# Twelve input-projection blocks taken in pairs by seven half-size products instead of eight

## The chip, the core and the metric

The kernel runs on one core of a Trainium2 chip. Its engines work side by side and are held together by semaphores: PE (TensorE, matrix products; PEld is its loading of the stationary operand), DVE (VectorE), ACT (ScalarE), POOL (GpSimd) and SP, which issues most DMA transfers. Products are written to PSUM, eight banks of 128 x 512 fp32; POOL has no part in PSUM. The metric is the device time of one execution in microseconds (us), as the median of several runs.

## The reference

A decoder layer on 1024 tokens of width 1024: one combined input projection feeds an mLSTM with 4 heads, dilated attention with 8 heads and cross-attention into 256 memory tokens with 4 heads; the outputs, gated by SiLU paths, are joined, projected, added to the input and normalised.

```python
hn = rmsnorm(x, g_norm)
proj = hn @ w_in                                   # 1024 x 6144
xm, zm, om, qa, ka, va, za, qx, zx = split(proj)   # 1024 x3, 512 x6
...
y_m = (head_layernorm(sigmoid(om) * mlstm(xm), g_head) + skip * xc) * silu(zm)
y_a = dilated_attention(rope(qa), rope(ka), va) * silu(za)
kx, vx = split(rmsnorm(mem, g_mem) @ w_mem_kv)
y_x = softmax(qx @ kx.T / sqrt(128)) @ vx * silu(zx)
return rmsnorm(x + concat([y_m, y_a, y_x]) @ w_out, g_final)
```

All is fp32. The blocks of this change are four of qx, four of zx and zm2 to zm5, each 128 columns of `w_in`.

## The kernel before

**Products in two parts.** An fp32 number is held as a high part in PE's format fp32r and the rest as a low part. `split` (line 80) makes them: ACT copies the high part (line 81), DVE or POOL subtracts (line 82; POOL for the blocks in `LO_ON_POOL`). A product is three matmuls: high by high, high by low, low by high.

**The input.** `x_in` (line 924) brings the transposed input in eight chunks of 128 channels (k) by 1024 tokens. For each chunk DVE makes the high part times `g_norm` (line 965) and the low part (line 966), kept in `hnh`, `hnl`; PE multiplies it with two weight blocks at once, zm6 and zm7 (lines 974 to 976), whose sums stay in four PSUM banks (`s1` three times, `po`); ACT squares it (line 981) and POOL adds the squares (line 982). `rms` (line 232) turns the sums into 1/rms, by columns (`rsx`) and along the free dimension (`rsb`), together with that of the memory tokens, which `mem_in` (line 994) prepares. The factor 1/rms by token is put on after the projections, where a block ends: `silu2` (line 247) multiplies with `rsb`, and makes SiLU by tanh.

**The stream.** Other blocks stand in a list, `stream` (line 118), in the order of lines 907 to 909. A block loads its weights one block ahead (`wload`, line 122, tags `wr`, `wh`, `wl` of two buffers each) and has pieces: a `ch_block` (line 181) has two, each 128 channels by 512 tokens, 24 matmuls of 512 columns into a `pj` bank (two banks, lines 167 to 169); a `t_block` (line 195) four, each 48 matmuls of 256 columns (lines 211 to 213). The loops of the stages pull pieces between their own steps, so that PE has work while a softmax runs: `fill(n)` pulls n pieces, `until(name)` all to the end of a block. `CROSS_FILLS`, `GOALS` and `HEAD_FILLS` set how many. qx and zx of head h come ahead of its cross attention (`qx_block`, `zx_block`), zm5 to zm2 under the last pair of attention heads, om0 and zm1 behind xm7, beside the gates.

**Stages in order.** Input; cross attention (8 units, `cross_scores`, `cross_values`) with the mLSTM's weights (`lstm_weight`, line 511); attention (16 units); the rest of xm; `gates` (line 619), a long chain on 4 partitions that ends in columns for the heads; the heads (8 units of `head_weights`, `head_values`, `head_out`); the output projection.

**The order of instructions.** Each engine works its queue in order. The order is made by the framework's planner, which plays the program through with estimated durations (line 1168, `schedule_with_timeline_sim`): earlier program text has priority, what is ready earlier may go ahead of it, `tc.high_priority` moves text forward. A tile with a tag takes one of the tag's buffers and waits until one is free: `g` (13 of 128 x 1024), `hn` (8 of 128 x 2 x 1024), `t2k` (4 of 128 x 512), `x4` (3).

## Time and profile before

| | |
|---|---|
| time, median of 3 runs | 1067.74 us (1067.39 to 1068.25) |
| span of the profiled execution, first to last instruction | 1062.8 us |
| time of that execution around its span | not in the page; the median is 4.9 us above the span |
| mean granted PE clock | 0.992 |
| matmuls | 6528 |
| moved by DMA | 117.03 MB, mean 110 GB/s |

How to read it: the page gives busy time by engine, 40 slices of the span with a digit for the busy tenths, the chain of work that ended last, and groups of instructions by line of the program, with what ended the idle time before them. A busy PE row holds matmuls that overlap, so the spacing of starts in the timeline says more than the duration of one. A wait is put down to the semaphore that came last.

### The profile page before, as it was taken

The numbers are of one execution on the slowest core, as the hardware profiler recorded it, in microseconds if no ns is written. First come the engines' busy times: TensorE is split into PE (matmuls) and PEld (weight loads), VectorE is DVE, ScalarE is ACT, GpSimd is POOL, SyncE is SP. The second block draws the span as 40 slices with busy tenths as digits, with TensorE's granted clock in tenths as the row PEclk, the third lists the DMA queues.
The fourth block names the chain that finished last, engine by engine and source line by source line (L and its number), as shares of the span: only waits on it lengthen the run. The fifth ranks groups of instructions, "written<-read, shape, count | busy, mean of one in ns | idle before, by whom it ended". The sixth has DMA issues, their size and how long they took to land.

```text
span 1062.8 us, 17259 instructions
## 1 busy us (share of the span) xinstructions
PE 1030.0 (97%) x6528; PEld 920.1 (87%) x6528; DVE 700.4 (66%) x1458; ACT 446.3 (42%) x876; POOL 309.8 (29%) x296
## 2 busy tenths in 40 slices
PE   6899999999999999999999999989999999999996
...
PEclk8899999999999999999999999999999999999999
...
GB/s 284 86 124 110 83 103 62 93 65 92 80 21 41 46 95 34 47 70 70 90 50 110 120 124 154 107 143 140 119 212 295 132 171 166 128 120 120 96 117 86
DMA packets 76435, 117.03 MB, mean 110 GB/s; under 512 B 14780, under 2 KB 46012, under 8 KB 76352
## 3 DMA queue, kind: packets, MB, share of 16 engines
...
HBM read 79.09 MB, written 31.57 MB: 104 GB/s over the span
## 4 chain that ended last, share of the span: by engine, by line
PE 78%; DVE 10%; DMA 6%; ACT 2%; issue 1%; POOL 1%; SPq 0%; POOLq 0%; DVEq 0%; ACTq 0%
PE pj L167 10%; PE pj L168 10%; PE pj L169 10%; PE pj L178 5%; PE pj L179 5%; PE pj L177 5%; PE pj L211 3%; PE pj L213 3%; PE pj L212 3%; PE tp L479 3%; DVE t2k L581 2%; DMA v<-P 2%; DMA wr<-in_w_out_dram 2%; PE s L454 2%; PE po L488 1%
## 5 line engine op out<-in xcount | busy, mean ns | idle before, releaser
L167 PE MATMUL pj<-hn,wh 128*128 128x512 f32 x544 | 216.8, 398 | 2.4 <-DVE t2k L249 1.3
L169 PE MATMUL pj<-hn,wl 128*128 128x512 f32 x544 | 217.0, 399 | 0.0
L168 PE MATMUL pj<-hn,wh 128*128 128x512 f32 x544 | 216.3, 398 | 0.0
L167 PEld LDWEIGHTS pj<-hn,wh 128*128 128x128 f32 x544 | 102.3, 188 | 25.6 <-DVE t2k L249 1.8
L81 ACT ACTIVATE wh<-wr 128x1024 fp32r<-128x1024 f32 x67 | 70.9, 1058 | 127.2 <-PE pj L168 53.8
L169 PEld LDWEIGHTS pj<-hn,wl 128*128 128x128 f32 x544 | 102.3, 188 | 22.7
L168 PEld LDWEIGHTS pj<-hn,wh 128*128 128x128 f32 x544 | 102.3, 188 | 22.3
L211 PE MATMUL pj<-wh,hn 128*128 128x256 f32 x384 | 107.9, 281 | 1.3 <-ACT st L262 1.3
L213 PE MATMUL pj<-wh,hn 128*128 128x256 f32 x384 | 107.5, 280 | 0.0
L212 PE MATMUL pj<-wl,hn 128*128 128x256 f32 x384 | 107.2, 279 | 0.0
L82 POOL TENSOR_TENSOR wl<-wr,wh 128x1024 fp32r<-128x1024 f32 x23 | 55.7, 2420 | 145.8 <-ACT wh L81 112.8
L82 DVE TENSOR_TENSOR wl<-wr,wh 128x1024 fp32r<-128x1024 f32 x44 | 57.0, 1296 | 46.5 <-ACT wh L81 34.9
L81 ACT ACTIVATE pth<-tp 128x512 fp32r<-128x512 f32 (+2 forms) x96 | 50.1, 540 | 73.3 <-PE tp L479 42.7
L82 DVE TENSOR_TENSOR ptl<-tp,pth 128x512 fp32r<-128x512 f32 (+2 forms) x96 | 58.0, 618 | 28.5 <-ACT pth L81 28.2
L211 PEld LDWEIGHTS pj<-wh,hn 128*128 128x128 f32 x384 | 72.1, 188 | 2.1 <-ACT st L262 1.5
L212 PEld LDWEIGHTS pj<-wl,hn 128*128 128x128 f32 x384 | 72.1, 188 | 0.4
L213 PEld LDWEIGHTS pj<-wh,hn 128*128 128x128 f32 x384 | 72.1, 188 | 0.2
L177 PE MATMUL pj<-wh,hn 128*128 128x256 f32 x256 | 71.9, 281 | 0.0
L178 PE MATMUL pj<-wl,hn 128*128 128x256 f32 x256 | 71.8, 280 | 0.0
L179 PE MATMUL pj<-wh,hn 128*128 128x256 f32 x256 | 71.7, 280 | 0.0
L462 ACT ACTIVATE P<-P,mx 128x128 f32<-128x128 f32 (+3 forms) x64 | 49.3, 772 | 21.1 <-DVE mx L458 20.8
L468 POOL TENSOR_SCALAR P<-P,ls 128x128 f32<-128x128 f32 (+4 forms) x40 | 29.2, 736 | 89.4 <-DVE ls L463 60.1
...
## 6 DMA issues: line engine op xcount, KB each, us to landing
...
```

The costliest lines, as they stand in the source:

```text
L81: S.activation(hi, src, AF.Copy)
L82: (eng_lo or V).tensor_tensor(lo, src, hi.bitcast(F32), op=SUB)
L167: PE.matmul(o, hi[:, ks], ah(k, cs), start=k == 0, stop=False)
L168: PE.matmul(o, hi[:, ks], al(k, cs), start=False, stop=False)
L169: PE.matmul(o, lo[:, ks], ah(k, cs), start=False, stop=k == KC - 1)
L177: PE.matmul(o, ah(k, cs), hi[:, ks], start=k == 0, stop=False)
L178: PE.matmul(o, ah(k, cs), lo[:, ks], start=False, stop=False)
L179: PE.matmul(o, al(k, cs), hi[:, ks], start=False, stop=k == nk - 1)
L211: PE.matmul(oi, hn_h(4 * kh + k, cs), hi[:, ks], start=kh == 0 and k == 0 and i == 0, stop=False)
L212: PE.matmul(oi, hn_h(4 * kh + k, cs), lo[:, ks], start=False, stop=False)
L213: PE.matmul(oi, hn_l(4 * kh + k, cs), hi[:, ks], start=False, stop=kh == 1 and k == 3 and i == 1)
L462: S.activation(pr, pr, AF.Exp, bias=mx, scale=-1.0, accum_out=ls)
```

## The change

Two blocks with the weights of 256 channels make a 2 x 2 of halves: A11, A12 are the first block's weights for channels k 0 to 511 and 512 to 1023, A21, A22 the second block's. The input is a 2 x 2 as well: B11, B12 are k 0 to 3 for tokens 0 to 511 and 512 to 1023, B21, B22 the same of k 4 to 7. The four results C = A B need eight half products of 4 k x 3 matmuls; Strassen's method (in Winograd's form) needs seven, of sums:

```
S1 = A21 + A22   S2 = S1 - A11   S3 = A11 - A21   S4 = A12 - S2
T1 = B12 - B11   T2 = B22 - T1   T3 = B22 - B12   T4 = B21 - T2
P1 = A11 B11  P2 = A12 B21  P3 = S4 B22  P4 = A22 T4  P5 = S1 T1  P6 = S2 T2  P7 = S3 T3
U2 = P1 + P6   U4 = U2 + P5
C11 = P1 + P2   C12 = U4 + P3   C21 = U2 + P7 + P4   C22 = U2 + P7 + P5
```

- The twelve blocks leave the stream; `pairs` runs them right behind the input as six units. `unit_load` brings a unit's weights, `unit_sums` makes S1 to S4 on POOL, `unit_split` splits a product's weights three products ahead, `product` runs 12 matmuls, `unit_step` recombines. P2 is added to P1's bank by PE, P4 to P7's, P3 to P5's (in unit 0 P3 stands second and has a bank of its own).
- `t_build` makes T1 to T4 of one k as its two chunks arrive; the chunks come in the order 0, 4, 1, 5, 2, 6, 3, 7. They take twelve `g` tiles and two `hn` tiles.
- The input's high parts are made by ACT; the squares go by halves.
- B12 isn't kept: `b12_again` loads it again behind the units.
- qx and zx go to DRAM, `cross_load` brings them back by head. `mem_in` and its `rms` come behind the units.
- zm0 goes from the place ahead of xm7 to cross attention, za0 too; om0 takes the place of zm5 to zm2. The fills and `LO_ON_POOL` are set anew.

```diff
 LO_ON_POOL = ("last", "om0", "om1", "out0_2", "out1_0", "out1_1", "out2_3", "qa0", "qa3", "va1", "xm3", "xm7",
-              "za1", "zm0", "zm1", "zm2", "zm4", "zm5", "zx0", "zx2")
+              "za1", "zm0", "zm1")
 NORM = "GGGGGVVV"
-CROSS_FILLS = (2, 3, 1, 3, 4, 1, 2, 2)
-HEAD_FILLS = [(4, 0), (2, 2), (2, 2), (3, 1), (3, 3), (4, 3), (3, 3), (0, 2), (2, 3)]
-GOALS = ("za1", "za2", "za3", "zm2")
+CROSS_FILLS = (1, 2, 2, 2, 2, 1, 1, 1)
+HEAD_FILLS = [(4, 0), (2, 2), (2, 2), (3, 1), (3, 3), (4, 3), (3, 2), (0, 2), (2, 3)]
+GOALS = ("za1", "za2", "za3", "om0")
...
+    b2 = [None] * 4
+    b1 = [[None] * 4, [None] * 4]
+    def hn_part(i, k, cs):
+        if k >= 4:
+            return b2[k - 4][:, i, cs]
+        c = cs.start // 512
+        return b1[c][k][:, i, cs.start - 512 * c:cs.stop - 512 * c]
     def hn_h(k, cs):
-        return hnh[k][:, cs]
+        return hn_part(0, k, cs)
     def hn_l(k, cs):
-        return hnl[k][:, cs]
...
-    def silu2(o, dst, half):
-        t = t2k()
-        V.tensor_tensor(t, o, rsb[:, half * 512:half * 512 + 512], op=MUL)
+    def silu2(o, dst, half, in_sbuf=False):
+        r = rsb[:, half * 512:half * 512 + 512]
+        if in_sbuf:
+            t = o
+            G.tensor_tensor(t, o, r, op=MUL)
+        else:
+            t = t2k()
+            V.tensor_tensor(t, o, r, op=MUL)
         S.activation(dst, t, AF.Tanh, scale=0.5)
         V.scalar_tensor_tensor(dst, dst, 1.0, t, op0=ADD, op1=MUL)
+    qx_d = [dram(f"qx{h}", [P, T]) for h in range(4)]
+    zx_d = [dram(f"zx{h}", [P, T]) for h in range(4)]
...
-    mh = [g4(F32R) for _ in range(2)]
+    mh, ml, kv = [], [], {}
+    def mem_tiles():
+        mh.extend(g4(F32R) for _ in range(2))
+        ml.extend(g4(F32R) for _ in range(2))
+        for n in ("kxh", "kxl", "vxh", "vxl"):
+            kv[n] = g4(F32R)
...
-    def qx_block(h):
-        def done(half, o):
...
-    def zx_block(h):
-        def done(half, o):
...
+    def cross_load(h):
+        xq[h] = (g4(F32R), g4(F32R))
+        for c in range(2):
+            hs = slice(c * 512, c * 512 + 512)
+            raw = t2k()
+            nc.sync.dma_start(raw, qx_d[h][:, hs])
+            split(xq[h][0][:, hs], xq[h][1][:, hs], raw)
+        xz[h] = g4()
+        nc.sync.dma_start(xz[h], zx_d[h])
...
-          "xm": xm_block, "kx": kx_block, "vx": vx_block, "qx": qx_block, "zx": zx_block}
-    for name in ("qx0 kx0 qx1 vx0 kx1 zx0 zx1 kx2 kx3 qx2 vx1 zx2 qx3 zx3 "
-                 "qa0 va0 ka0 ka1 za0 qa1 za1 va1 qa2 ka2 za2 qa3 ka3 za3 zm5 zm4 zm3 zm2 "
-                 "xm0 xm1 xm2 xm4 xm3 xm5 xm6 zm0 xm7 om0 zm1 om1 om3 om2").split():
+          "xm": xm_block, "kx": kx_block, "vx": vx_block}
+    for name in ("kx0 vx0 kx1 zm0 kx2 kx3 vx1 za0 "
+                 "qa0 va0 ka0 ka1 qa1 za1 va1 qa2 ka2 za2 qa3 ka3 za3 om0 "
+                 "xm0 xm1 xm2 xm4 xm3 xm5 xm6 xm7 zm1 om1 om3 om2").split():
...
+    tq = [[None] * 4 for _ in range(4)]
     def x_in():
-        ws = [[], []]
+        xs = {}
+        wraw = [tagged("wr", [P, 1024], F32, 2) for _ in range(2)]
...
+        order = [0, 4, 1, 5, 2, 6, 3, 7]
+        for n, k in enumerate(order):
+            xs[k] = g4() if n < 4 or n == 5 else x4([P, T])
+            if n < 2:
                 for c in range(2):
...
+                    nc.sync.dma_start(xs[k][:, c * 512:c * 512 + 512], xt[k * P:(k + 1) * P, c * 512:c * 512 + 512])
+                    wpart(c, n)
             else:
                 nc.sync.dma_start(xs[k], xt[k * P:(k + 1) * P, :])
...
+            if n == 3:
+                nc.sync.dma_start(ident, c_id)
+                unit_load(0)
...
+        h1 = [h8(F32R) for _ in range(2)]
+        t4s = [h8(F32R) for _ in range(2)]
+        for n, k in enumerate(order):
             g = col(G_NORM, k)
...
+            x = xs[k]
+            if k < 4:
+                b1[0][k] = h1[k // 2].rearrange("p i (a b) -> p i a b", a=2)[:, k % 2]
+                b1[1][k] = g4(F32R).rearrange("p (a b) -> p a b", a=2)
+                for c in range(2):
+                    xc_ = x[:, c * 512:c * 512 + 512]
+                    S.activation(b1[c][k][:, 0, :], xc_, AF.Copy, scale=g)
+                    V.scalar_tensor_tensor(b1[c][k][:, 1, :], xc_, g, b1[c][k][:, 0, :].bitcast(F32),
+                                           op0=MUL, op1=SUB)
+            else:
+                b2[k - 4] = h8(F32R)
+                S.activation(b2[k - 4][:, 0, :], x, AF.Copy, scale=g)
+                V.scalar_tensor_tensor(b2[k - 4][:, 1, :], x, g, b2[k - 4][:, 0, :].bitcast(F32), op0=MUL, op1=SUB)
             for w in range(2):
...
+            if n == 0:
+                S.activation(acc, x, AF.Square)
             else:
...
+                for c in range(2):
+                    cs = slice(c * 512, c * 512 + 512)
+                    sq = tagged(("P4", "P5")[c], [P, 512])
+                    S.activation(sq, x[:, cs], AF.Square)
+                    G.tensor_tensor(acc[:, cs], acc[:, cs], sq, op=ADD)
+            if k >= 4:
+                t_build(k - 4, xs[k - 4], x, t4s)
+        with tc.high_priority(offset=60):
+            rms(acc, rsx, ((0, 4, rsb[:, :512]), (4, 4, rsb[:, 512:])))
...
+    def t_build(k, xa, xb, t4s):
+        ga, gb = col(G_NORM, k), col(G_NORM, k + 4)
+        x11, x12, x21, x22 = xa[:, :512], xa[:, 512:], xb[:, :512], xb[:, 512:]
+        for i in range(3):
+            tq[i][k] = g4(F32R).rearrange("p (a b) -> p a b", a=2)
+        tq[3][k] = t4s[k // 2].rearrange("p i (a b) -> p i a b", a=2)[:, k % 2]
+        d, e = t2k(), t2k()
+        G.tensor_tensor(d, x12, x11, op=SUB)
+        G.tensor_scalar(e, x12, ga, None, op0=MUL)
+        t3, t2 = t2k(), t2k()
+        V.scalar_tensor_tensor(t3, x22, gb, e, op0=MUL, op1=SUB)
+        V.scalar_tensor_tensor(t2, x11, ga, t3, op0=MUL, op1=ADD)
+        t4 = tagged("zs", [P, 512], F32, 2)
+        V.scalar_tensor_tensor(t4, x21, gb, t2, op0=MUL, op1=SUB)
+        T1 = tq[0][k]
+        S.activation(T1[:, 0, :], d, AF.Copy, scale=ga)
+        V.scalar_tensor_tensor(T1[:, 1, :], d, ga, T1[:, 0, :].bitcast(F32), op0=MUL, op1=SUB)
+        split(tq[2][k][:, 0, :], tq[2][k][:, 1, :], t3, G)
+        split(tq[1][k][:, 0, :], tq[1][k][:, 1, :], t2)
+        split(tq[3][k][:, 0, :], tq[3][k][:, 1, :], t4)
+    def b12_again():
+        h2 = [h8(F32R) for _ in range(2)]
+        for k in range(4):
+            raw = t2k()
+            nc.sync.dma_start(raw, xt[k * P:(k + 1) * P, 512:])
+            g = col(G_NORM, k)
+            d = b1[1][k] = h2[k // 2].rearrange("p i (a b) -> p i a b", a=2)[:, k % 2]
+            S.activation(d[:, 0, :], raw, AF.Copy, scale=g)
+            V.scalar_tensor_tensor(d[:, 1, :], raw, g, d[:, 0, :].bitcast(F32), op0=MUL, op1=SUB)
+    def zm_done(j):
+        def done(half, o, in_sbuf):
+            st = st2()
+            silu2(o, st, half, in_sbuf)
+            nc.sync.dma_start(zm_d[j][half], st)
+        return done
...
+    def qx_done(h):
+        def done(half, o, in_sbuf):
+            if not in_sbuf:
+                st = st2()
+                S.activation(st, o, AF.Copy)
+                o = st
+            nc.sync.dma_start(qx_d[h][:, half * 512:half * 512 + 512], o)
+        return done
+    units = [((40, qx_done(0)), (44, zx_done(0))), ((10, zm_done(2)), (11, zm_done(3))),
+             ((41, qx_done(1)), (45, zx_done(1))), ((12, zm_done(4)), (13, zm_done(5))),
+             ((42, qx_done(2)), (46, zx_done(2))), ((43, qx_done(3)), (47, zx_done(3)))]
+    raws, sums, wps, keep = {}, {}, {}, {}
+    def unit_load(u):
+        raws[u] = []
+        for i in range(2):
+            raw = tagged("wr", [P, 1024], F32, 2) if u % 2 == 0 else x4([P, 1024])
+            nc.sync.dma_start(raw, w_all[units[u][i][0]])
+            raws[u].append(raw)
+    def unit_sums(u):
+        (ra, rb) = raws[u]
+        a11, a12, a21, a22 = ra[:, :512], ra[:, 512:], rb[:, :512], rb[:, 512:]
+        s1_, s2_, s3_ = [tagged(t, [P, 512]) for t in ("P3", ("P4", "P6")[u % 2], "P5")]
+        s4_ = tagged("zs", [P, 512], F32, 2)
+        G.tensor_tensor(s1_, a21, a22, op=ADD)
+        G.tensor_tensor(s2_, s1_, a11, op=SUB)
+        G.tensor_tensor(s3_, a11, a21, op=SUB)
+        G.tensor_tensor(s4_, a12, s2_, op=SUB)
+        sums[u] = {1: a11, 2: a12, 4: a22, 5: s1_, 6: s2_, 7: s3_, 3: s4_}
+    nwp = [0]
+    def unit_split(u, p):
+        t = tagged(("wh", "wl")[nwp[0] % 2], [P, 1024], F32R, 2)
+        nwp[0] += 1
+        split(t[:, :512], t[:, 512:], sums[u][p])
+        wps[u, p] = t
+    def product(u, p, o, first):
+        t = wps.pop((u, p))
+        h0, h1_ = slice(0, 512), slice(512, 1024)
+        rhs = {1: lambda i, k: hn_part(i, k, h0), 2: lambda i, k: hn_part(i, k + 4, h0),
+               3: lambda i, k: hn_part(i, k + 4, h1_), 4: lambda i, k: tq[3][k][:, i, :],
+               5: lambda i, k: tq[0][k][:, i, :], 6: lambda i, k: tq[1][k][:, i, :],
+               7: lambda i, k: tq[2][k][:, i, :]}[p]
+        for k in range(4):
+            hi, lo = t[:, k * P:(k + 1) * P], t[:, 512 + k * P:512 + (k + 1) * P]
+            PE.matmul(o, hi, rhs(0, k), start=first and k == 0, stop=False, skip_group_check=True)
+            PE.matmul(o, hi, rhs(1, k), start=False, stop=False, skip_group_check=True)
+            PE.matmul(o, lo, rhs(0, k), start=False, stop=k == 3, skip_group_check=True)
+    def unit_step(u, p):
+        m = keep.setdefault(u, {})
+        (_, done1), (_, done2) = units[u]
+        early = u == 0
+        if p == 1:
+            m["a"] = pj()
+            product(u, 1, m["a"], True)
+            m["p1"] = tagged("ptl", [P, 512], F32, 2)
+            S.activation(m["p1"], m["a"], AF.Copy)
+        elif p == 2:
+            product(u, 2, m["a"], False)
+            done1(0, m["a"], False)
+        elif p == 6:
+            m["b"] = s1()
+            product(u, 6, m["b"], True)
+            m["u2"] = tagged("pth", [P, 512], F32, 2)
+            V.tensor_tensor(m["u2"], m["b"], m["p1"], op=ADD)
+        elif p == 5:
+            m["c"] = s1()
+            product(u, 5, m["c"], True)
+            m["u4"] = tagged("ptl", [P, 512], F32, 2)
+            V.tensor_tensor(m["u4"], m["c"], m["u2"], op=ADD)
+            if early:
+                t = t2k()
+                V.tensor_tensor(t, m["u4"], m["p3"], op=ADD)
+                done1(1, t, True)
+        elif p == 7:
+            product(u, 7, m["b"], True)
+            t = t2k()
+            V.tensor_tensor(t, m["b"], m["u4"], op=ADD)
+            done2(1, t, True)
+        elif p == 3:
+            if early:
+                o = pj()
+                product(u, 3, o, True)
+                m["p3"] = tagged("pth", [P, 512], F32, 2)
+                S.activation(m["p3"], o, AF.Copy)
+            else:
+                product(u, 3, m["c"], False)
+                t = t2k()
+                V.tensor_tensor(t, m["c"], m["u2"], op=ADD)
+                done1(1, t, True)
+        else:
+            product(u, 4, m["b"], False)
+            t = t2k()
+            V.tensor_tensor(t, m["b"], m["u2"], op=ADD)
+            done2(0, t, True)
+    def pairs():
+        seq = []
+        for u in range(len(units)):
+            seq += [(u, p) for p in ((1, 3, 2, 6, 5, 7, 4) if u == 0 else (1, 6, 2, 5, 7, 3, 4))]
+        unit_sums(0)
+        ahead = 3
+        for n in range(ahead):
+            unit_split(*seq[n])
+        for n, (u, p) in enumerate(seq):
+            if n % 7 == 1 and u + 1 < len(units):
+                unit_load(u + 1)
+            if n % 7 == 3 and u + 1 < len(units):
+                unit_sums(u + 1)
+            if n + ahead < len(seq):
+                unit_split(*seq[n + ahead])
+            unit_step(u, p)
+    def mem_in():
+        mts = [g4() for _ in range(2)]
+        for i in range(2):
+            nc.sync.dma_start(mts[i], memt[i])
...
+        rms(sq[0], rsm, ((0, 2, rsmb),))
     nc.sync.dma_start(chv_s, chv)
     V.tensor_scalar(chv_s[:, :, 2:9], chv_s[:, :, 2:9], 0.5, None, op0=MUL)
     x_in()
+    pairs()
+    mem_tiles()
+    mem_in()
+    b12_again()
...
-    until("qx1")
     for n, (h, half) in enumerate(units):
+        if half == 0:
+            cross_load(h)
         if prev is not None:
             ph = units[n - 1][0]
             until(f"vx{ph // 2}")
-            until(f"zx{ph}")
             cross_values(*units[n - 1], prev)
         until(f"kx{h}")
-        until(f"qx{h}")
         prev = cross_scores(h, half)
-        if n == 6:
+        if n == 1:
             tables()
         lw[n]()
         fill(CROSS_FILLS[n])
```

More of the change, by code (lines that the diff above doesn't have):

```diff
@@ L317, in hymba_kernel @@
     xq, xz = {}, {}
-    def qx_block(h):
-        def done(half, o):
-            if half == 0:
-                xq[h] = (g4(F32R), g4(F32R))
-            hs = slice(half * 512, half * 512 + 512)
-            split(xq[h][0][:, hs], xq[h][1][:, hs], o)
-        ch_block(f"qx{h}", 40 + h, done)
-    def zx_block(h):
-        def done(half, o):
-            if half == 0:
-                xz[h] = g4()
-            silu2(o, xz[h][:, half * 512:half * 512 + 512], half)
-        ch_block(f"zx{h}", 44 + h, done)
+    def cross_load(h):
[7 more added lines that the diff above has]
+        nc.sync.dma_start(xz[h], zx_d[h])
     def cross_scores(h, half):
```

99 lines of the change are left out of this document (33 added, 66 removed).

## The prediction

> **What bounds the kernel now.** I read the page first, then the waits of PE, then busy time by stage, then the timeline of the first 60 us.
>
> ```profile
> span 1062.8 us, 17259 instructions
> PE 1030.0 (97%) x6528; PEld 920.1 (87%) x6528; DVE 700.4 (66%) x1458; ACT 446.3 (42%) x876; POOL 309.8 (29%) x296
> PE   6899999999999999999999999989999999999996
> PEclk8899999999999999999999999999999999999999
> PE 78%; DVE 10%; DMA 6%; ACT 2%; issue 1%; POOL 1%; SPq 0%; POOLq 0%; DVEq 0%; ACTq 0%
> ...
> PE s L974 <- DVE hn L965: 5.1, 2, 3.3
> PE s L975 <- DVE hn L966: 4.2, 2, 2.9
> PE s L706 <- DVE t2k L714: 2.0, 1, 2.0
> ...
> 0.00:45.34 45.34, 33.01 (x106) 24.05 (x107) 39.97 (x35) 19.03 (x25) 31.02 (x29) 0.85 0.57 170
> 45.34:210.00 164.66, 164.66 (x944) 142.93 (x943) 92.61 (x201) 64.10 (x140) 39.33 (x49) 1.00 0.33 104
> 250.00:325.00 75.00, 74.56 (x423) 63.79 (x421) 54.04 (x132) 40.16 (x86) 36.11 (x39) 1.00 0.22 56
> 400.00:475.00 75.00, 72.50 (x378) 59.71 (x377) 60.78 (x148) 46.38 (x99) 31.87 (x34) 1.00 0.18 46
> ```
>
> PE is busy in 97% of the span and carries 78% of the chain that ended last. The waits say where it is not: the two longest sums, 5.1 and 4.2 us, belong to lines 974 and 975, the products made while the input arrives; behind them no PE wait is over 2.0 us. In the rows by stage (length, then PE, PEld, DVE, ACT, POOL, clock, DMA share, GB/s) PE is full from 45.34 to 210 us, and DVE is nearest to taking over in attention (60.78 of 75 us at 400 to 475). So after 45 us a matmul removed is time removed, as long as nothing new makes PE wait. Up to 45 us it is not: there PE waits for DVE.
>
> **What a removed matmul is worth.** The mean of a 128x512 matmul in the page is 398 ns, but matmuls overlap, so the spacing of their starts counts.
>
> ```profile
> 45.57 0.39 PE L167 MATMUL pj<-hn,wh 128*128 128x512 f32 x1
> ...
> 49.30 0.39 PE L169 MATMUL pj<-hn,wl 128*128 128x512 f32 x1
> ```
>
> These are the first and the last of 17 consecutive matmuls: (49.30 - 45.57) / 16 = 0.233 us. A pair of blocks is 2 x 48 = 96 of them, 22.4 us. Seven products of 4 k x 3 = 12 are 84, 19.6 us. So a pair saves 12, six pairs 72, and 72 x 0.233 = **16.8 us**. PE gets no new work: sums and recombination are on DVE, ACT and POOL. One sentence by a page: the Trainium skill, "TensorE: Matmul & The Clock Gate" (Back-to-back issue gap), gives about 131 ns a matmul as the sustained spacing at N=512, by which the saving would be 9.4 us. This trace disagrees with 0.233 us, and the measurement decides.
>
> **The start, where I pay.** The rows that matter:
>
> ```profile
> 9.82 0.75 DVE L965 TENSOR_SCALAR hn<-g,chv_s 128x1024 fp32r<-128x1024 f32 x1
> 10.61 1.28 DVE L966 SCALAR_TENSOR_TENSOR hn<-g,chv_s,hn 128x1024 fp32r<-128x1024 f32 x1
> 10.94 17.61 POOL L982 TENSOR_TENSOR P<-P,x 128x1024 f32<-128x1024 f32 x6 [8.72 <-ACT x L981]
> 14.63 2.83 DVE L965 TENSOR_SCALAR hn<-g,chv_s 128x1024 fp32r<-128x1024 f32 x1
> 17.49 3.27 DVE L966 SCALAR_TENSOR_TENSOR hn<-g,chv_s,hn 128x1024 fp32r<-128x1024 f32 x1
> 28.51 7.28 POOL L513 TENSOR_TENSOR P<-tw,bdm 128x128 f32<-128x128 f32 x7
> 45.33 0.39 PE L976 MATMUL po<-hn,t2k 128*128 128x512 f32 x1
> ...
> L966 DVE SCALAR_TENSOR_TENSOR hn<-g,chv_s,hn 128x512 fp32r<-128x512 f32 x2 | 1.5, 752 | 0.1
> L584 DVE SCALAR_TENSOR_TENSOR g<-t2k,t2k 128x512 f32<-128x512 f32 x1 | 0.7, 693 | 0.7 <-ACT t2k L583 0.7
> L82 POOL TENSOR_TENSOR wl<-wr,wh 128x1024 fp32r<-128x1024 f32 x23 | 55.7, 2420 | 145.8 <-ACT wh L81 112.8
> L427 POOL TENSOR_TENSOR t2k<-t2k,t2k 128x512 f32<-128x512 f32 x8 | 10.4, 1296 | 0.2
> L391 POOL TENSOR_TENSOR t2k<-t2k,x 128x512 f32<-128x512 f32 x16 | 24.0, 1502 | 44.9 <-ACT t2k L384 44.9
> L468 POOL TENSOR_SCALAR P<-P,ls 128x512 f32<-128x512 f32 x8 | 6.1, 760 | 4.7 <-DVE ls L463 4.7
> L85 POOL TENSOR_TENSOR rs<-rs,nhalf 128x10 f32<-128x10 f32 x1 | 2.0, 1982 | 0.2 <-DVE rs L239 0.2
> ```
>
> The same DVE operation on SBUF takes 0.75 us ahead of POOL's additions and 2.83 us among them; six additions take 17.61 us, 2.94 each. DVE gets about one operation in per POOL operation. That, not PE, set the 45.33 us at which the last input product starts; its 96 matmuls are 22.4 us of PE.
>
> Removed here: DVE's high halves (7 of 1024, two of 512) go to ACT, which is busy 19.03 of 45.34 us, and the memory tokens' preparation goes behind the pairs. Added: `t_build` with 6 DVE and 3 POOL operations for each of four k, the sums of unit 0 (4 on POOL), and seven weight splits.
>
> DVE until unit 0 is done: 4 weight halves, 8 `b1`, 24 of `t_build`, 7 splits, 43 of 512 at 0.72 (between 0.693 and 0.752), and 4 `b2` of 1.28: 36.1 us. POOL: 14 half additions, 8 of `t_build` and 4 sums, 26 at 1.30; 4 tensor_scalar at 0.76; the power at 1.98: 38.8 us. POOL starts at 10.94 as before. Between DVE operations each of its 30 is lengthened by 0.2 us (L391 against L427) to 0.5 us (2.94 against the 2.42 of the 1024 form): 45 to 54 us, so POOL ends at 56 to 65 us.
>
> What PE needs of that comes late. Unit 0 runs products 1, 3, 2, 6, 5, 7, 4. Product 3 needs the last of the four sums, product 6 the last k of `t_build`, and a PSUM bank that only the RMS chain frees. If the planner puts the sums early into POOL's gaps (as it put the L513 operations of a later part at 28.51), product 6 starts some 1.5 us (two DVE operations) behind POOL's end, 57.5 to 66.5, and four products of 2.8 us end at 69 to 78. If the sums come last, product 3 starts there, and six products end at 74 to 83. Undisturbed it would be 45.3 + 19.6 = 65. So the start costs +4 to +18 us. A gain isn't excluded: were DVE not held by POOL at all, its 36.1 us from 9.8 on would end at 46 and the last four products at 57, a gain of 8. I take 73, a cost of **+8**: sums early, POOL's stretch in the middle.
>
> Two queues get new waits. The squares on ACT go into `P4` and `P5`, one buffer each, so a square waits for POOL's addition of the chunk before, and behind it on ACT stand the next chunk's high halves, for which PE waits; this is POOL's pace again, counted above. On SP the raw weights of unit 0 stand in the program ahead of the last four chunks and wait for the `wr` buffers of the first two blocks; chunks a few us later are hidden by POOL's 45 us or more.
>
> **Units 1 to 5.** The rows for ACT here and for the memory tokens:
>
> ```profile
> L81 ACT ACTIVATE pth<-tp 128x512 fp32r<-128x512 f32 x64 | 36.7, 592 | 49.7 <-PE tp L479 30.0 <-PE tp L367 11.0 <-PE po L487 7.8
> ...
> 23.98 2.09 ACT L1000 ACTIVATE g<-g,chv_s 128x256 fp32r<-128x256 f32 x5
> ```
>
> 19.6 us of PE each. DVE for a zm pair: 7 weight halves, 3 additions that end an output, 2 into `u2` and `u4`, one product with `rsb`, 4 closing ones of `silu2`, 17 x 0.69 = 11.7 us. POOL: 4 sums, 3 products with `rsb`, 9.1 us. ACT: 7 x 0.59 for halves, 5 for copies and tanh, about 7 us. Each fits alone; the 11 DVE operations on two SBUF tiles (7.6 us) and POOL's 9.1 do so one after the other too, 16.7 of 19.6. But PSUM is used twice: product 4 adds to the bank from which the sum of product 7 must first be read, with only product 3 (2.8 us) between, and the same for 5 and 3, and 1 and 2. A read that finds DVE at a split which itself waits for a POOL operation comes after 1.30 + 0.69 + 0.69 = 2.7 us: just in time, so 0 to about 1 us for each of 4 handovers in 5 units, 0 to 20. Most will find DVE free: **+2**.
>
> **Covers taken away.** Twelve blocks leave the stream that filled PE under cross attention and attention.
>
> ```profile
> L349 DVE TENSOR_REDUCE mx<-s 128x2 f32<-128x512 f32 x16 | 10.8, 682 | 3.4 <-PE s L347 3.4
> L354 ACT ACTIVATE g<-s,mx,rsq 128x256 f32<-128x256 f32 x32 | 17.6, 560 | 12.2 <-DVE mx L351 10.8 <-DVE t2k L374 1.3
> L358 DVE TENSOR_SCALAR g<-g,ls 128x256 f32<-128x256 f32 x32 | 9.2, 349 | 0.2
> ...
> 658.91 0.68 ACT L632 ACTIVATE x<-s,bg 4x512 f32<-4x512 f32 x1
> 688.10 0.72 ACT L652 ACTIVATE g<-g,P 4x512 f32<-4x512 f32 x1 [0.41 <-DVE g L651]
> ...
> 950.00:1000.00 50.00, 50.00 (x427) 50.00 (x427) 23.94 (x44) 8.13 (x8) 13.01 (x6) 1.00 0.32 106
> ```
>
> In cross attention a unit's chain from its last score is 0.68 + 2 x 0.56 + 4 x 0.35 = 3.2 us and some handovers; the smallest fill, half a block of 24 matmuls, is 5.6 us: nothing. In attention the first pair loses 11 us of fill and the last 22 (eight zm pieces of 5.6 out, four om pieces of 48 at 50 / 427 = 0.117, 5.6, in). DVE at 54 of 75 us becomes about 51 of 64: below PE. Gates: from 658.91 to 688.10 runs a chain that om0 and zm1 (22.5 + 11.2 us) cover. Now zm1 and, if the planner draws it ahead past `head_weights`, om1 (22.5) stand there; without om1 some 15 us of wait. In before it drew om0 ahead of xm7's tail, so I expect it to. The new stores and loads of qx and zx, some 8 MB, find DMA at a third. Moving the memory tokens costs at most the 3.4 us of 8 ACT copies of 0.42, beside five products: nothing. Together **+1**, from 0 to 15.
>
> **Sum.** -16.8 + 8 + 2 + 1 = -5.8 us. The page gives the profiled execution's span, 1062.8, and no more; the runs' median, 1067.7, is 4.9 above, which I keep. So the span becomes 1057.0 and the time **1062 us**.
>
> **Rivals.**
> 1. DVE and POOL take the start over: sums last, stretch 0.5, unit 0 done at 83 or later. For: both were full from 10 to 45 us before, and get more operations. Against: less of DVE's work stands ahead of the input products. From an end at 65 + 16.8 - 3 = 79 us on, all is lost; at 85 the time is 1067.7 - 16.8 + 20 + 3 = 1074. Slower.
> 2. The handovers of PSUM stall in units 1 to 5, 0.6 us each of 20: 12 instead of 2, 1072.
> 3. om1 isn't drawn ahead: 15 us of wait at the gates, 1077. Against: the order around xm7.
> 4. The clock falls. The slow rows:
>
> ```profile
> 20.00:30.00 10.00, 4.98 (x12) 3.18 (x12) 10.00 (x5) 7.75 (x13) 9.84 (x5) 0.67 0.66 112
> 21.41 0.63 PE L976 MATMUL s<-hn,ptl 128*128 128x512 f32 x1
> 21.83 0.63 PE L975 MATMUL s<-hn,pth 128*128 128x512 f32 x1
> ...
> 34.83 0.39 PE L974 MATMUL s<-hn,t2k 128*128 128x512 f32 x1
> ```
>
> While PE starved the granted clock was 0.67, and matmuls started 0.42 us apart. If PE idles ahead of product 6, its last four products (48) at 0.42 cost 48 x 0.19 = 9 us more: 1071. The Trainium skill, "TensorE: Matmul & The Clock Gate" (The HAM clock gate), has the array at half clock after an idle window of some 3.4 us until it was busy for as long; by that only about 3.4 us run slow, 1.6 us lost, 1064. The trace agrees so far: the short duration, 0.39 us, is back at 34.83 us, once PE ran on.
> 5. The change saves less than its count (0.131 us a matmul, the page's spacing): 1069.5. The rows above are against it.
>
> **Chances.** Forecast 0.56, rivals 0.18, 0.08, 0.08, 0.07, 0.03. A measurement of this kernel tells 0.2% (2.1 us) from no change. Of the forecast a little lies within 2.1 us of 1067.7, of rivals 2 and 4 a share: faster 0.54, same 0.17, slower 0.29. The range takes in the full saving with a gain at the start (-16.8 - 3, 1048) and most of rivals 1 and 3: 1048 to 1080.
>
> **What would show it.** Right: 72 fewer 128x512 matmuls at 0.233 us; unit 0's product 4 done near 73 us, with DVE and POOL full until then; 98 us of PE for units 1 to 5 with under 5 us of wait; om1's matmuls ahead of the gates' transposes. Wrong: an end of unit 0 beyond 79 us, PE waits on `u2`, `u4` or the sums' additions, a wait of over 5 us for the gates' columns.

## The result: 6% slower, and where the time went

The changed kernel takes 1136.45 us (1134.31 to 1138.14) where the kernel before took 1067.99 us in the same series: ratio 1.0619, 95% interval 1.0584 to 1.0654. The forecast was 1062, the range ended at 1080. From the page of the changed kernel, the span, PE's busy time, PE and its clock in 40 slices, and the chain that ended last:

```profile
span 1134.2 us, 17491 instructions
PE 1047.0 (92%) x6456; PEld 925.3 (82%) x6456; DVE 767.5 (68%) x1532; ACT 489.5 (43%) x956; POOL 376.2 (33%) x349
PE   7769999899899999999999899649999999999996
PEclk8879999999898999999999899869999999999998
PE 55%; DVE 8%; DMA 6%; ACT 2%; issue 1%; POOL 1%; POOLq 0%; DVEq 0%; ACTq 0%
```

The 72 matmuls are gone (6528 to 6456). But PE carries 55% of the chain where it carried 78%, and the slices show new holes: near 60 us, and in slices 26 and 27, around 720 to 770 us. PE's waits (engine, line, releaser: us in total, times, longest):

```profile
PE pj L700 <- ACT g L81: 8.7, 1, 8.7
PE po L608 <- DVE g L612: 6.4, 2, 3.8
PE pj L701 <- DVE g L82: 5.8, 1, 5.8
PE tp L243 <- POOL P L1005: 5.1, 1, 5.1
PE s L995 <- ACT g L983: 5.0, 2, 3.9
PE pj L167 <- DVE x L588: 3.8, 2, 3.3
```

Line 588 takes a half block of xm out of PSUM, lines 608 and 612 make the values and the gates' inputs from it; 700 and 701 are the first head behind the gates. The windows of the same stages, changed kernel first (length, then PE, PEld, DVE, ACT, POOL, clock, DMA share, GB/s):

```profile
90.00:186.00 96.00, 96.00 (x425) 78.20 (x424) 68.18 (x86) 37.30 (x63) 52.12 (x37) 1.00 0.32 110
186.00:215.00 29.00, 22.41 (x143) 19.57 (x141) 23.62 (x42) 16.21 (x35) 12.16 (x10) 0.94 0.60 207
285.00:307.00 22.00, 17.85 (x109) 15.07 (x108) 14.35 (x35) 8.75 (x26) 7.16 (x11) 0.84 0.29 78
640.00:720.00 80.00, 72.22 (x336) 58.31 (x336) 62.23 (x114) 35.20 (x64) 9.59 (x10) 0.96 0.38 109
720.00:766.00 46.00, 21.76 (x76) 16.10 (x77) 35.51 (x55) 22.49 (x34) 6.36 (x7) 0.67 0.37 104
```

and the kernel before:

```profile
75.00:250.00 175.00, 175.00 (x1036) 153.43 (x1036) 93.12 (x203) 66.69 (x152) 40.54 (x52) 1.00 0.29 87
552.00:652.00 100.00, 98.68 (x484) 81.73 (x484) 82.48 (x151) 44.94 (x83) 11.79 (x12) 1.00 0.43 126
652.00:690.00 38.00, 36.98 (x271) 34.60 (x270) 28.87 (x32) 21.93 (x34) 10.35 (x8) 1.00 0.37 113
```

In the rest of xm DVE was busy 82 of 100 us before. From attention's last product to xm's last that stage takes 110.6 us before, with 108.4 us of matmuls, and 105.5 now, with 77.7: with om0 and zm0 beside it PE was full; without them 31 us less of matmuls shorten it by 5 us, PE waits for DVE (lines 588 and 612), and in the window across its end (720 to 766 us, which takes in the gates) the clock falls to 0.67.

To compare stages, count PE's matmuls at their undisturbed spacing in the trace of the kernel before (0.233 us for 512 columns, 0.118 for 256, 0.175 for 384, 0.12 and less for the rest). What is left of a stage's length is **lost**: waits and slow clock. The 8.7 us in which PE stands behind xm's last product, ahead of line 700, count to the gates; some 9 us behind PE's last matmul, alike in all five, are left out. The same for three runs below:

| lost, us | before | changed | e1 | e6 | e7 |
|---|---|---|---|---|---|
| to the first cross score | 22.1 | 44.5 | 23.8 | 30.6 | 45.2 |
| cross attention | 0.6 | 16.9 | 16.8 | 0.7 | 17.5 |
| attention | 13.7 | 21.2 | 20.2 | 13.3 | 20.9 |
| rest of xm | 2.2 | 27.9 | 26.9 | 21.6 | 4.0 |
| to the gates' columns | 1.2 | 18.5 | 18.8 | 21.5 | 7.2 |
| heads, output | 10.8 | 9.5 | 11.2 | 10.4 | 12.8 |
| PE's matmuls | 1003.3 | 986.6 | 1003.3 | 1003.3 | 992.2 |

In the changed kernel 41.4 us are lost when unit 0's 84 matmuls are through, at 87.0 us, 40.8 at the end of the units (186.4 us), and 3.7 more to the first cross score.

### The profile page after: what moved, and what is told of

Read it like the earlier page. It is cut to its first block, busy times and chain, and to the rows that moved or that the text cites. A ratio compares the mean times of both kernels' runs of the same rounds, so it can differ in the third digit from the quotient of the medians.

```text
span 1134.2 us, 17491 instructions
## 1 busy us (share of the span) xinstructions
PE 1047.0 (92%) x6456; PEld 925.3 (82%) x6456; DVE 767.5 (68%) x1532; ACT 489.5 (43%) x956; POOL 376.2 (33%) x349
## 4 chain that ended last, share of the span: by engine, by line
PE 55%; DVE 8%; DMA 6%; ACT 2%; issue 1%; POOL 1%; POOLq 0%; DVEq 0%; ACTq 0%
PE pj L167 5%; PE pj L168 5%; PE pj L169 5%; PE pj L178 4%; PE pj L179 4%; PE pj L177 4%; PE pj L211 3%; PE pj L212 3%; PE pj L213 3%; DMA v<-P 3%; PE tp L490 2%; DMA wr<-y 2%; DVE t2k L592 2%; DMA wr<-in_w_out_dram 2%; PE s L465 1%; PE po L499 1%
## 5 line engine op out<-in xcount | busy, mean ns | idle before, releaser
L167 PE MATMUL pj<-hn,wh 128*128 128x512 f32 x352 | 143.6, 408 | 5.6 <-DVE x L588 3.8
L169 PE MATMUL pj<-hn,wl 128*128 128x512 f32 x352 | 142.7, 405 | 0.0
L168 PE MATMUL pj<-hn,wh 128*128 128x512 f32 x352 | 142.0, 403 | 0.0
L81 ACT ACTIVATE wh<-wr 128x1024 fp32r<-128x1024 f32 (+1 forms) x66 | 65.0, 986 | 121.2 <-PE pj L179 55.7
L213 PE MATMUL pj<-wh,hn 128*128 128x256 f32 x384 | 108.4, 282 | 0.0
L167 PEld LDWEIGHTS pj<-hn,wh 128*128 128x128 f32 x352 | 67.6, 192 | 21.8 <-DVE x L588 4.5
L82 POOL TENSOR_TENSOR wl<-wr,wh 128x1024 fp32r<-128x1024 f32 x18 | 44.6, 2480 | 114.3 <-ACT wh L81 68.4
L169 PEld LDWEIGHTS pj<-hn,wl 128*128 128x128 f32 x352 | 67.6, 192 | 15.0
L82 DVE TENSOR_TENSOR wl<-wr,wh 128x1024 fp32r<-128x1024 f32 (+1 forms) x39 | 51.1, 1311 | 42.5 <-ACT wh L81 42.5
L168 PEld LDWEIGHTS pj<-hn,wh 128*128 128x128 f32 x352 | 67.3, 191 | 14.6
L82 DVE TENSOR_TENSOR g<-t2k,g 64x512 fp32r<-64x512 f32 (+3 forms) x80 | 55.5, 719 | 12.9 <-ACT g L81 12.1
```

Source lines behind the costliest of these rows:

```text
L81: S.activation(hi, src, AF.Copy)
L82: (eng_lo or V).tensor_tensor(lo, src, hi.bitcast(F32), op=SUB)
L167: PE.matmul(o, hi[:, ks], ah(k, cs), start=k == 0, stop=False)
L168: PE.matmul(o, hi[:, ks], al(k, cs), start=False, stop=False)
L169: PE.matmul(o, lo[:, ks], ah(k, cs), start=False, stop=k == KC - 1)
L213: PE.matmul(oi, hn_l(4 * kh + k, cs), hi[:, ks], start=False, stop=kh == 1 and k == 3 and i == 1)
```

## Experiments on the blocks' place

**e1: the twelve blocks plain at the pairs' place**, no T's, no weight sums. The changed input, the way of qx and zx through DRAM and the second load of B12 stay.

```diff
-            if k >= 4:
-                t_build(k - 4, xs[k - 4], x, t4s)
...
-        for n, (u, p) in enumerate(seq):
...
-            unit_step(u, p)
+        for n, (_, done) in enumerate(blocks):
+            nxt = load(n + 1) if n + 1 < len(blocks) else None
+            for half in range(2):
+                o = pj()
+                proj_ch(w, hn_h, hn_l, half * 512, 512, o)
+                done(half, o, False)
+            w = nxt
```

> The twelve blocks stay where the change put them, but each is computed as before, eight half products for two blocks, without the sums T1 to T4 and S1 to S4; results still go via DRAM. Theory A (the stages that lost their fill make the loss): PE waits behind the units stay, some 70 us in cross attention, attention, the xm blocks and the gates; the start falls back from about 41 us of lost PE time to about 22, PE work rises by 16.8: about 1134 us. Theory B (the extra work of the sums, or the twelve g tiles that T takes, causes the later waits too): below 1080 us.

1131.3 us, ratio 1.0569 (1.0537 to 1.0602), as theory A has it. The loss behind the units is there without any half product. What Strassen's method adds at this place is small: by the traces it saves 16.7 of PE and loses 44.5 - 23.8 = 20.7 more ahead of the first cross score, and the two ratios' intervals overlap.

**e6: zm5 to zm2 moved to the front, om0 into their place**, in the kernel before.

```diff
-    for name in ("qx0 kx0 ...
+    for name in ("zm5 zm4 zm3 zm2 qx0 kx0 ...
-                 "... za3 zm5 zm4 zm3 zm2 "
-                 "xm0 ... xm6 zm0 xm7 om0 zm1 ...
+                 "... za3 om0 "
+                 "xm0 ... xm6 zm0 xm7 zm1 ...
-GOALS = ("za1", "za2", "za3", "zm2")
+GOALS = ("za1", "za2", "za3", "om0")
```

> The kernel before with blocks moved and nothing else: zm5 to zm2 run plain right behind the input, om0 takes their place under the last attention heads; qx, zx, zm0 and za0 stay. Theory cover (a stage bound by DVE and handovers needs the moved blocks beside it): the last pair has 22.5 us of fill for 45, the rest of xm loses om0, the gates too: 25 to 40 us more, 1093 to 1108. Rival (the blocks' place is free; the loss in the changed kernel comes from the way of qx and zx through DRAM, from the memory tokens' late place or from the order of the heads): within 4 us of before, 1064 to 1072.

1113.1 us, 1.0427 (1.0406 to 1.0448): 45 us for moving blocks, more than expected. All blocks are computed as in the kernel before, and the way of qx and zx and the memory tokens' place are unchanged. Its tail, window and wait:

```profile
716.00:745.00 29.00, 12.18 (x47) 9.31 (x47) 18.40 (x19) 13.60 (x18) 6.12 (x6) 0.65 0.34 101
```

```profile
PE pj L689 <- ACT g L81: 10.7, 1, 10.7
```

PE is busy 12 of 29 us beside the gates, at a clock of 0.65; line 689 is the first head, as 700 in the changed kernel. (8.5 us of the 45 lie ahead of cross attention. PE waits there 3.8 us for line 249, the end of a zm block, which needs `rsb`, and 2.3 for line 1006, the squares of the memory tokens; in the kernel before the first is 1.3 and the second isn't there.)

**e7: zm5 to zm2 back**, in the changed kernel; four units are left.

```diff
-              "za1", "zm0", "zm1")
+              "za1", "zm0", "zm1", "zm2", "zm4", "zm5")
...
-GOALS = ("za1", "za2", "za3", "om0")
+GOALS = ("za1", "za2", "za3", "zm2")
...
-                 "... za3 om0 "
-                 "xm0 ... xm7 zm1 ...
+                 "... za3 zm5 zm4 zm3 zm2 "
+                 "xm0 ... xm7 om0 zm1 ...
...
-    units = [((40, qx_done(0)), (44, zx_done(0))), ((10, zm_done(2)), (11, zm_done(3))),
-             ((41, qx_done(1)), (45, zx_done(1))), ((12, zm_done(4)), (13, zm_done(5))),
+    units = [((40, qx_done(0)), (44, zx_done(0))), ((41, qx_done(1)), (45, zx_done(1))),
```

> The changed kernel with four units only (qx with zx): zm5 to zm2 plain under the last attention heads and om0 behind xm7, as before; cross attention as changed. Theory cover: of the 69 us of the change the about 50 lost in attention, the rest of xm and the gates are gone, the saving is 11.2 for 16.8: 1085 to 1100. Rival (those stages lose by what comes ahead of them): above 1120.

1110.1 us, 1.0398 (1.0378 to 1.0419), between the two expectations. The rest of xm and the gates lose 11.2 us instead of 46.4, as the cover theory has it; attention (20.9 for 21.2) didn't follow, so its loss had another cause.

**e15: za0 alone moved**, from the first pair of heads to ahead of attention, in the kernel before.

```diff
-    ... zx3 qa0 va0 ka0 ka1 za0 qa1 ...
+    ... zx3 za0 qa0 va0 ka0 ka1 qa1 ...
```

> The kernel before with za0 ahead of the attention stage instead of under its first heads, nothing else. Theory cover: the first pair loses 11.2 us of PE work beside its chains, attention grows by 5 to 9 us, 1073 to 1077. Rival (attention's longer time in the changed kernel has another cause): within 2.5 us, 1066 to 1070.

1077.0 us against 1070.4, 1.0067 (1.0052 to 1.0082); attention loses 20.5 us instead of 13.7. That is attention's part.

**e3 and e4: the tail.** e3 puts the first fill of the heads (om1's four pieces) ahead of `head_weights`; e4 puts om0 back behind xm7.

```diff
+        if n == 0:
+            fill(HEAD_FILLS[n][0])
         a = head_weights(u)
-        fill(HEAD_FILLS[n][0])
+        if n > 0:
+            fill(HEAD_FILLS[n][0])
```

```diff
-GOALS = ("za1", "za2", "za3", "om0")
+GOALS = ("za1", "za2", "za3", "za3")
...
-                 "... za3 om0 "
-                 "xm0 ... xm7 zm1 ...
+                 "... za3 "
+                 "xm0 ... xm7 om0 zm1 ...
```

> The text of the four om1 pieces goes ahead of head_weights of the first head; nothing else. If om1 came late only because its text stood behind head_weights, which takes pj banks first, the wait at the gates (17 us more than before) falls below 4 us: about 1119 us. If its weights come late, or the xm chain itself holds everything, no more than 4 us are gained: above 1131 us.

> om0 goes back behind xm7, the last pair of attention heads gets no fill in its place; the six units stay. Theory A, tail: the waits from the last attention unit to the gates' columns (44 us more than before) fall to 10 or less, the last attention pair loses 0 to 20: 1101 to 1122 us. If DVE and ACT hold the xm blocks by themselves, the waits ahead of the gates stay: above 1128 us.

e3: 1124.1, 1.0503 (1.0472 to 1.0533), between its two expectations; om1 now runs beside the gates. e4: 1136.0, 1.0614 (1.0580 to 1.0647), no gain: the rest of xm loses 17.1 for 27.9 and the gates some 13 for 18.5, but attention 35.8 for 21.2, because om0 had been the fill of its last heads. So e4 falls into the range of its second expectation by another way. In the changed kernel's timeline the reason that om1 came late is to be seen:

```profile
744.23 0.40 PE L623 MATMUL s<-ptl,g 128*128 128x512 f32 x1
753.35 1.32 PE L700 MATMUL pj<-g,wvg 128*128 128x512 f32 x2 [8.72 <-ACT g L81]
760.45 0.80 PE L701 MATMUL pj<-g,wvg 128*128 128x512 f32 x1 [5.79 <-DVE g L82]
...
766.61 0.28 PE L211 MATMUL pj<-wh,hn 128*128 128x256 f32 x1
```

Both `pj` banks belong to the head's products of lines 700 and 701, which come first in the text and wait for their operands; om1 (line 211) writes to `pj` too and gets a bank only behind them. That the text's order was the cause e3 shows; that the banks were is a reading of these rows.

**e11: zm0 ahead of kx0**, in the changed kernel, to fill 186 to 215 us.

```diff
-    for name in ("kx0 vx0 kx1 zm0 kx2 ...
+    for name in ("zm0 kx0 vx0 kx1 kx2 ...
```

> The changed kernel with zm0 ahead of kx0 in the stream instead of behind kx1. From 187 to 215 us PE lost some 11 us while DVE was full with the memory tokens and the first head's splits. Theory entry (nothing stands beside that chain): zm0's 11.2 us stand there, 6 to 11 us less, 1125 to 1130. Rival (cross attention has too little fill in all; the gap opens where zm0 stood): within 3 us of the changed kernel, 1133 to 1139.

1140.1, 1.0648 (1.0600 to 1.0697): no gain. 18.9 us are lost from the units' end to attention, 20.6 in the changed kernel; the gap moves. The memory tokens, which the expectation saw in that gap, were done by then: in the changed kernel their sums (lines 1201 to 1203) end on DVE at 179.8 us, under the units. From 186 to 215 us DVE has the low parts of B12 (line 1049, four operations between 191.9 and 201.0), of weights and of the first head, and the first softmax. Cross attention has 22 us of blocks left beside it, zm0 and za0, where it had the 90 us of qx and zx.

## Experiments on the start

**e2: neither T's nor weight sums. e13: weight sums, no T's.** In both, products 4 to 7 take the input's own halves; e2 takes the raw weights too.

```diff
-            if k >= 4:
-                t_build(k - 4, xs[k - 4], x, t4s)
...
+        if p > 3:
+            rhs = [lambda i, k: hn_part(i, k + 4, h0), lambda i, k: hn_part(i, k + 4, h1_)][p % 2]
...
-        sums[u] = {1: a11, 2: a12, 4: a22, 5: s1_, 6: s2_, 7: s3_, 3: s4_}
+        sums[u] = {1: a11, 2: a12, 4: a22, 5: a21, 6: a21, 7: a11, 3: a12}
```

The last two lines, and the sums' four additions, are e2's alone.

> Seven products a unit stay, but neither T1 to T4 nor S1 to S4 is computed: products 4 to 7 take parts of the input and of the raw weights as they are, so six of the twelve results are not the reference's. Theory A: only the start gains, unit 0 ends near 65 us in place of 84.5 and everything behind it keeps its waits: about 1136 - 19 = 1117 us. If the order of the input, ACT's high parts or the squares by halves set the start, unit 0 ends after 78 us: 1130 us or more. Theory B: below 1080 us.

> The changed kernel without t_build: products 4 to 7 take B21 and B22 in place of the T's (six of the results are not the reference's), the weight sums stay. Theory T (their 36 operations on DVE, POOL and ACT are the start's price): as without both, unit 0 done by 62, 1110 to 1117. Theory S (the weight sums at POOL's end are the price): unit 0 at 75 or later, 1125 to 1137.

e2: 1112.3, 1.0392 (1.0358 to 1.0425), 12.9 us lost when unit 0 is through, at 58.6 us. e13: 1122.7, 1.0492 (1.0458 to 1.0525), 22.9 lost, at 68.5, between its two expectations. So the S's cost 10 us of the start and the T's, 41.4 less 22.9, 18.5.

**e14: POOL out of `t_build`.**

```diff
-        G.tensor_tensor(d, x12, x11, op=SUB)
-        G.tensor_scalar(e, x12, ga, None, op0=MUL)
+        V.tensor_tensor(d, x12, x11, op=SUB)
+        S.activation(e, x12, AF.Copy, scale=ga)
...
-        split(tq[2][k][:, 0, :], tq[2][k][:, 1, :], t3, G)
+        split(tq[2][k][:, 0, :], tq[2][k][:, 1, :], t3)
```

> The changed kernel with POOL out of t_build: the difference d and T3's low part on DVE, the scaled half e on ACT; the sums are the same. Theory POOL (its stretch, and DVE's turns with it, set the start): POOL is some 20 us lighter until 60 us, DVE 6 us heavier; unit 0 done at 72 to 78, 1121 to 1128. Rival (ACT's and DVE's own work or their waits on each other set it): within 4 us of the changed kernel, 1132 to 1140.

1130.7, 1.0566 (1.0531 to 1.0601), an interval that overlaps the changed kernel's, between its two expectations; unit 0 is through at 82.9. From 20 to 60 us DVE has no pause, in e14 as without the change:

```profile
20.00:40.00 20.00, 13.50 (x49) 9.56 (x48) 20.00 (x17) 9.93 (x17) 14.78 (x10) 0.91 0.28 29
40.00:60.00 20.00, 14.76 (x44) 11.34 (x43) 20.00 (x21) 9.42 (x16) 11.50 (x7) 0.67 0.31 101
```

What POOL is spared, DVE gets.

**e8, e9, e10: the weight sums ahead.** Unit 0's S2 and S3 use the buffers P4 and P5 of the squares, so they stand behind the last square. e9 gives S2 another buffer (P6), makes S3 in A21's place and moves the sums ahead. e10 also gives product 6 a `tp` bank. e8 had S4 in an `st` buffer.

```diff
-        unit_sums(0)
+        with tc.high_priority(offset=300):
+            unit_sums(0)
...
-        s1_, s2_, s3_ = [tagged(t, [P, 512]) for t in ("P3", ("P4", "P6")[u % 2], "P5")]
+        s1_ = tagged("P3", [P, 512])
+        s2_ = tagged(("P6" if u == 0 else ("P4", "P6")[u % 2]), [P, 512])
+        s3_ = a21 if u == 0 else tagged("P5", [P, 512])
...
-                m["b"] = s1()
+                m["b"] = tp() if early else s1()
```

> The changed kernel; unit 0's S2, S3 and S4 get buffers that the squares don't use (P6, A21's own place, an st buffer) and go ahead on POOL. Theory sums (product 3's wait for S4 is the start's price): unit 0 done near 75 instead of 87, 1124 to 1128. Rival (the price is the RMS chain behind POOL's additions, which frees the bank of product 6; product 2 only moves ahead of it): at most 3 us, 1133 or more.

> The changed kernel; unit 0's S2 goes to P6 and S3 to A21's own place, so that they don't wait for the squares' buffers P4 and P5; S4 keeps its zs buffer (in the run before, the st buffer made it wait for the RMS chain); the sums go ahead on POOL. Theory sums (product 3's wait for S4 is the start's price): unit 0 done near 75 instead of 87, 1124 to 1128. Rival (the RMS chain, which frees the bank of product 6, is the price; product 3 and 2 only move ahead of it): unit 0 done at 84 or later, 1132 or more.

> As the one before, and product 6 of unit 0 takes a tp bank instead of one that the RMS chain frees. If sums and bank together are the start's price, products 1, 3, 2 and 6 run without a stop to about 66 and only product 5 waits for the RMS chain: unit 0 done at 76 to 81, 1126 to 1131. If it is the T's (POOL and DVE by turns on SBUF), no more than 3 us better than the one before.

e8: 1154.8, 1.0817 (1.0788 to 1.0847); it tested something else, because the `st` buffer was still held by a store:

```profile
80.92 1.26 POOL L1102 TENSOR_TENSOR st<-wr,P 128x512 f32<-128x512 f32 x1 [10.87 <-DMA zm<-st]
```

e9: 1145.8 (two runs, 9 us apart), 1.0702 (1.0636 to 1.0767), unit 0 through at 91.5. e10: 1136.9, 1.0618 (1.0574 to 1.0663), at 89.5. Neither order nor bank was the price. In e10 the sums are early, and the squares end at 67.0 instead of 63.3, the RMS chain with them:

```profile
58.75 8.29 POOL L1005 TENSOR_TENSOR P<-P,P 128x512 f32<-128x512 f32 x5
...
74.24 1.67 POOL L85 TENSOR_TENSOR rs<-rs,nhalf 128x8 f32<-128x8 f32 x1
```

PE needs both ends of the same POOL queue; whichever goes first, the other is late.

## Experiments on the input, and a faster kernel

In e1 and e2 the input's products had ended at 33.5 and 34.9 us instead of 45.6. Three kernels take that part alone into the kernel before. **e5**: ACT makes the high halves. **e12**: and the squares are added by halves. **e16**: and POOL makes the low half of qx0's weights.

```diff
-                V.tensor_scalar(hnh[k][:, c0:c1], xs[k][:, c0:c1], g, None, op0=MUL)
+                S.activation(hnh[k][:, c0:c1], xs[k][:, c0:c1], AF.Copy, scale=g)
...
-                G.tensor_tensor(acc, acc, sq, op=ADD)
+                    G.tensor_tensor(acc[:, cs], acc[:, cs], sq, op=ADD)
...
-LO_ON_POOL = ("last", "om0",
+LO_ON_POOL = ("last", "qx0", "om0",
```

> The kernel before, with one thing of the change: ACT makes the input's high halves instead of DVE. Seen so far: with the twelve blocks computed plain at the place of the pairs, the input's products ended at 33.5 us, before at 45.6. Theory ACT (DVE's nine high halves were the start's price before): the input ends near 35 and the time falls by 8 to 12 us, 1056 to 1060. Rival (the chunk order or POOL's half-size additions did it, POOL's six additions of 2.94 us still hold DVE's low halves): within 3 us of before, 1065 to 1071.

> The kernel before with ACT making the input's high halves and the squares added by halves of 512 on POOL (two buffers, P4 and P5), no block moved. Theory pace (DVE gets one operation in per POOL operation, so shorter additions let it go faster): the input ends at 33 to 35 instead of 37.7, 1055 to 1058. Rival (DVE's pace no longer counts once ACT makes the high halves, the squares wait for two buffers only): 1059 to 1063.

> The kernel before with ACT making the high halves, the squares added by halves, and the low half of qx0's weights made by POOL, so that it doesn't stand behind the memory tokens on DVE (where PE waited 7.6 us for it). Theory: the input ends at 32 to 33 and PE runs on, the lead of 13 us less POOL's 2 to 3: 1056 to 1060, below the 1060.5 of the run with ACT alone. Rival (the RMS chain or the next block's low half is late instead): 1062 to 1069.

e5: 1060.5, **0.9943 (0.9922 to 0.9964)**, faster than both kernels; the input ends at 37.7. e12: the input ends at 32.2, yet 1069.1 against 1070.3, 0.9988 (0.9967 to 1.0008), slower than both its expectations. Its waits and DVE's timeline show who took the lead of 13 us:

```profile
PE pj L169 <- DVE wl L82: 7.6, 1, 7.6
```

```profile
27.83 6.92 DVE L1003 SCALAR_TENSOR_TENSOR g<-g,chv_s,g 128x256 fp32r<-128x256 f32 x8
34.67 2.29 DVE L1006 TENSOR_TENSOR x<-x,x 128x1024 f32<-128x1024 f32 x1
36.99 1.63 DVE L1007 TENSOR_TENSOR x<-x 128x512 f32<-128x512 f32 x1
38.55 2.28 DVE L82 TENSOR_TENSOR wl<-wr,wh 128x1024 fp32r<-128x1024 f32 x1
```

The next block's low half stood on DVE behind the memory tokens (lines 1003 to 1007); from 38 to 48 us the clock was 0.61. With it on POOL that wait is 2.3 us, and e16 takes 1062.7 against 1070.4, **0.9915 (0.9883 to 0.9947)**: above the 1056 to 1060 that were expected, but what the input's new way is worth, with no block moved. e5 and e16 can't be told apart.

## Why the prediction was wrong, step by step

- **The saving: right.** 72 matmuls at 0.233 us; PE's work is 1003.3 - 986.6 = 16.7 us less.
- **The start: +8 forecast, 41.4 - 22.1 = +19.3 measured.** "I take 73": it was 87. Rival 1 had the end at 83 or later, with the sums last, and they were:

```profile
58.84 4.51 POOL L1005 TENSOR_TENSOR P<-P,P 128x512 f32<-128x512 f32 x3 [0.65 <-ACT P L1004]
63.31 1.26 POOL L1097 TENSOR_TENSOR P<-P,wr 128x512 f32<-128x512 f32 x1
...
69.02 2.12 POOL L85 TENSOR_TENSOR rs<-rs,nhalf 128x8 f32<-128x8 f32 x1
```

  But e9 and e10 show that sums ahead wouldn't have helped, so the size failed, not an order. The POOL work that the sum lists came to 51.8 us, within the 45 to 54, although the four tensor_scalar took 2.00 to 2.54 us (the row's ns: shortest, median, longest) and not the 0.76 of L468. What the sum put at nothing are POOL's pauses, 9.9 us until the power has ended, in which it stood behind DVE and ACT, and 3.5 us of other work among it (line 524, the next unit's first sum):

```profile
L1027 POOL TENSOR_SCALAR t2k<-x,chv_s x2: 1997/2268/2539, 26.2 to 42.4; 128x512 f32<-128x512 f32 x2
```

```profile
23.89 2.34 POOL L1026 TENSOR_TENSOR t2k<-x 128x512 f32<-128x512 f32 x1 [2.56 <-DVE g L1035]
53.08 1.74 POOL L82 TENSOR_TENSOR g<-t2k,g 128x512 fp32r<-128x512 f32 x1 [3.75 <-ACT g L81]
```

  DVE was busy 39.8 of the 40 us from 20 to 60. POOL began at 5.9 us: 5.9 + 51.8 + 3.5 + 9.9 = 71.1, where 56 to 65 was forecast. And product 6 started at 75.9, not 1.5 but 4.8 us behind POOL's end: the transposes of 1/rms (line 249) start at 73.2, behind product 3, and line 259 must empty the bank. With 11.1 us for four products that makes 87.0. Rival 4's clock is there as well, ahead of product 3:

```profile
62.18 3.57 PE L243 MATMUL tp<-ones,P 128*128 128x1 f32 x16 [5.13 <-POOL P L1005]
67.74 0.79 PE L1119 MATMUL pj<-hn,wl 128*128 128x512 f32 x1 [1.98 <-ACT wl L81]
...
70.73 0.63 PE L1119 MATMUL pj<-hn,wl 128*128 128x512 f32 x1
71.16 0.63 PE L1120 MATMUL pj<-hn,wl 128*128 128x512 f32 x1
...
75.90 0.50 PE L1119 MATMUL s<-g,wl 128*128 128x512 f32 x1 [1.66 <-DVE t2k L259]
```

  Behind that pause product 3 ran at (71.16 - 70.73) = 0.43 us a matmul, at a granted clock of 0.50 from 66 to 73 us, so its twelve cost 12 x 0.20 = 2.4 us more. The four products from 75.9 on ran at 0.23 us a matmul, with the clock at 1.00 from 77 to 88 us: the 9 us of rival 4 didn't come. The Trainium skill, "TensorE: Matmul & The Clock Gate" (Wait — 56ns, not 53.3ns?), gives 426.7 ns as the spacing of cold matmuls of 512 columns; the trace agrees with 0.43.
- **Units 1 to 5: +2 forecast, -0.6 measured.** PE is full from 90 to 186 us; the handovers of PSUM cost nothing.
- **"Together +1, from 0 to 15" for the covers: the step that failed.** It was 97.7 - 28.5 = +69.2: from the units' end to the first cross score and in cross attention 20.6 - 0.6 = 20.0, attention 7.5, rest of xm 25.7, gates 17.3, heads -1.3. The working compared a unit's chain with a fill of 5.6 us and DVE with PE as busy shares; it never summed a stage's PE work without its blocks. In the rest of xm that sum is 78 us, and the stage takes 105.5. The prediction held attention for the stage where DVE is nearest to taking over (60.78 of 75 us, 0.81); the row of 552 to 652 us, shown above, has 82.48 of 100, and that is the rest of xm. The step looked at the gates alone there: zm0 went to cross attention and om0 under attention, so the rest of xm gave its own cover away, and the prediction has no price for that. The first pair's missing 11 us, which it held to be below PE's bound, cost 6.6 (e15). `b12_again`, whose low parts stand on DVE in the gap of 186 to 215 us, has no price in it either. The memory tokens did cost nothing, as forecast: they were prepared while PE was full.
- **"I expect it to" draw om1 ahead: wrong.** What kept om1 back is the order of the text (e3), not time. Rival 3 priced that at 15; the gates lose 17.3 more than before, which stands in the 69.2, and e3 gives back 12.

In sum -16.7 + 19.3 - 0.6 + 69.2 = +71.2, the spans' 1134.2 - 1062.8 = 71.4; the medians are 68.5 apart (the 4.9 us from span to median, which the forecast adds, are 2.3 in the changed kernel). By e6, e15 and the table the place alone makes some 45 + 7 + 16 in zm's blocks, za0 and cross attention, less the 12 us by which the input ends earlier in e1: 56 of e1's 61, a rough sum of pieces from different runs. Not tried: qx and zx moved without their way through DRAM, so that the 16 us of cross attention are argued from e1, e11 and the windows, not shown by an edit of their own. Against the way through DRAM speaks that from 200 to 340 us no wait of PE is put down to a DMA, and that ACT waits for the loads of qx 2.2 us in all.
